# Folding the token mix of the low-rank terms into their weights in an RWKV-7 and stick-breaking decoder

## The chip, the cores and the metric

One core of one Trainium2 chip. The metric is the device time of one execution in microseconds (us). Engines are named as the profile names them: PE (TensorE matmul), PEld (TensorE weight load), DVE (VectorE), ACT (ScalarE), POOL (GpSimd), SP (the engine that issues most transfers).

## The reference

A two-layer decoder on 1040 tokens (16 meta tokens and 1024 of the input) of width 1024. Layer 0 mixes tokens by RWKV-7, layer 1 by stick-breaking attention; a conv-gated MLP follows each. Only the first step of RWKV-7 is touched by the change:

```python
xx = token_shift(x) - x                       # x: (1040, 1024), normed
xr, xw, xk, xv, xa, xg = [x + xx * mix[i] for i in range(6)]
r = xr @ w_r;  k = xk @ w_k;  v = xv @ w_v    # 1024 x 1024 each
w_log = -softplus(-(w0 + tanh(xw @ w1) @ w2)) - 0.5     # w1: 1024 x 64
a = sigmoid(a0 + (xa @ a1) @ a2)                        # a1: 1024 x 64
g = sigmoid(xg @ g1) @ g2                               # g1: 1024 x 160
```

Each `mix[i]` has one number per channel. The terms of `w1`, `a1` and `g1` are called the low-rank terms here.

## The kernel before

Everything is float32. A product is made of three matmuls in a faster 4-byte format: each operand is split into a high part (an ACT copy into that format) and a low part (a subtraction, on DVE or POOL), and high x high, high x low and low x high are summed in PSUM. Activations lie with channels on the 128 partitions, so 1024 channels are eight blocks (`kt` = 0 to 7), and tokens along the free axis.

`rwkv_project` runs first. It treats the tokens in two segments (`SEGS`): 528 tokens (s = 0; products in two column halves of 264) and 512 (s = 1; one product of 512 columns). `phase0` loads the input, turns it and norms it: the normed blocks of segment 0 stay in SBUF with a zero column ahead (`hn0`), and all go to DRAM (`hn_s`), from where a block with the token before it can be read back (`load_hs`, L332). `norms(1)` and `normed(1)` do the same for segment 1; the latter is called in the midst of the mixing of segment 0 (L758).

For each segment `Mixer` (L339) then makes 48 mixed and split inputs, in the order of `mix_jobs` (L404): first 24 for the low-rank terms (for each kt the mixes 1, 4 and 5, that is w, a, g), then eight each for k, r and v. It is a pipeline of jobs: a load of the block six jobs ahead where it is not there (L362), for the way "d" a POOL subtraction that gives the difference of neighbouring tokens (L369, once per block), a DVE operation that multiplies it by the mix and adds h (L381), an ACT copy to the high part (L391, recorded at L76), and a subtraction for the low part on DVE or POOL (L396). For the way "a" an ACT copy scaled by 1 - mix (L374) and a DVE operation (L386) take the place of L369 and L381. Of the low-rank jobs 12 have their low part on DVE and 12 on POOL; of the others 15 on DVE and 9 on POOL.

`lora_in` (L421) splits the low-rank weights (`split_w`, `weights`), and as each job of the 24 is done, `step` issues its matmuls (L453): three for each column half, for w into 64 rows, for a into 64, for g into 128 and, from the second part of `g1`, 32. That is 192 matmuls of 264 columns in segment 0 and 96 of 512 in segment 1. `finish` (L467) applies tanh and sigmoid and splits the results.

Then `first_pair` (L700) makes the mixes of k, r and v and, of eight pairs of heads (128 output columns each), the first: `proj` (L543) for k, r and v, 48 matmuls each in segment 0 and 24 in segment 1, and the second low-rank products (`lora_wa`, `lora_g`). Pairs 1 to 7 follow (`pair`, L669), each beside `stage_e` (L565) of the pair before, which turns k, r, v, w, a into the operands of the recurrence with DVE, ACT, POOL and a few matmuls. `stage_e` of pair 7 of segment 0 runs beside the low-rank part of segment 1 (`next(e)`, L756). In the last pair of segment 0, `tick` (L767) lets the mixer of segment 1 make two steps at each of four places.

What sets the order: all matmuls that go through `pmm` stay in program order on PE. The other engines' queues are ordered by a planner at build time, and buffers are rings by tag: tag "M" holds 24 mixed and split inputs (k, r and v of a segment need all 24 until its last pair), tag "H" 22 vectors of 529 columns, and the tags "wf", "wh" and "wl" two blocks of weights each. After the projections (near 645 us of the span) come the recurrence, the rest of layer 0, layer 1 and the output, which the change does not touch.

Of the kernel before, what the change touches and what calls it, by code (L numbers as in the profile page):

```python
# [51 lines left out]
def kernel(ctx: ExitStack, tc: tile.TileContext, a: dict, out: bass.AP):  # L52
# [141 lines left out]
    NS = 528  # L194
    NC = 8
# [14 lines left out]
    def rwkv_project(ap, pa):  # L210
# [24 lines left out]
        def phase0():  # L235
# [5 lines left out]
            def big(name, n):  # L241
                return ap.tile([P, 2 * NS], F32, tag="M", bufs=24, name=name)[:, 0:n]

# [95 lines left out]
        class Mixer:  # L339
# [10 lines left out]
            def advance(self):  # L350
# [12 lines left out]
                if at(3):  # L363
                    nm, i, kt, via, sub = self.jobs[t + 3]
                    hs = self.hs[nm, kt]
                    if via == "d":
                        if (nm, kt) not in self.dd:
                            dd = H(f"dd{s}{nm}{kt}")[:, 0:n]
                            G.tensor_tensor(dd, hs[:, 0:n], hs[:, 1 : n + 1], op=ALU.subtract)  # L369
                            self.dd[nm, kt] = dd  # L370
                    else:
                        x = H(f"mt{s}{i}{kt}")[:, 0:n]
                        m = i * 8 + kt
                        S.activation(x, hs[:, 1 : n + 1], AF.Copy, scale=der[:, m : m + 1])  # L374
                        self.st[t + 3]["x"] = x
                if at(2):
                    nm, i, kt, via, sub = self.jobs[t + 2]
                    hs, st, m = self.hs[nm, kt], self.st[t + 2], i * 8 + kt
                    if via == "d":
# [7 lines left out]
                if at(1):  # L387
                    nm, i, kt, via, sub = self.jobs[t + 1]
                    st = self.st[t + 1]
                    st["xm"] = xm = ap.tile([P, 2, NS], F32R, tag="M", bufs=24, name=f"xm{s}{i}{kt}")  # L390
                    copy_act(xm[:, 0, 0:n], st["x"])  # L391
                if at(0):
# [3 lines left out]
                    sub.tensor_tensor(xm[:, 1, 0:n], st["x"], f(xm[:, 0, 0:n]), op=ALU.subtract)  # L396
# [24 lines left out]
        def lora_in(s, out):  # L421
# [3 lines left out]
            W = {}  # L425
            acc = {}

            def weights():
                wf = WP["pool"].tile([P, KT, P], F32, tag="wf", name=f"wf_wa{s}")
                nc.sync.dma_start(wf[:, :, 0:64], wview(a["rw_w1"][0], 0, 64))  # L430
                nc.sync.dma_start(wf[:, :, 64:128], wview(a["rw_a1"][0], 0, 64))
                W["wa"] = split_w(wf, P, f"wa{s}")
                wf = WP["pool"].tile([P, KT, P], F32, tag="wf", name=f"wf_g1{s}")
                nc.sync.dma_start(wf, wview(a["rw_g1"][0], 0, P))
                W["g"] = split_w(wf, P, f"g1{s}")
                wf = WP["pool"].tile([P, KT, 32], F32, tag="wf", name=f"wf_g1b{s}")
                nc.sync.dma_start(wf, wview(a["rw_g1"][0], P, 32))
                gh = ap.tile([P, KT, 32], F32R, tag="g1bh", name=f"g1bh{s}")
                gl = ap.tile([P, KT, 32], F32R, tag="g1bl", name=f"g1bl{s}")
                with behind(*begun) if s == 0 else nullcontext():  # L440
                    copy_act(gh, wf)
                    V.tensor_tensor(gl, wf, f(gh), op=ALU.subtract)
                W["gb"] = (gh, gl)
                fs = [ps_l] * 4 if len(hv) == 1 else [ps_l] * 4 + [ps_d] * 3 + [ps_n]
                for c0, cn in hv:
                    for nm in "wagb":
                        acc.setdefault(nm, []).append(fs.pop(0)(f"p{nm}{s}{c0}"))

            def add(nm, m, w, m0, X, kt):
                wh, wl = W[w]  # L450
                for h, (c0, cn) in enumerate(hv):
                    for j, (ww, xx) in enumerate(((wh, X[0]), (wh, X[1]), (wl, X[0]))):
                        pmm(  # L453
                            acc[nm][h][0:m, 0:cn], ww[:, kt, m0 : m0 + m], xx[:, c0 : c0 + cn],
                            start=kt == 0 and j == 0, stop=kt == KT - 1 and j == 2,
                        )

            def step(i, kt, X):
                if i == 1:
                    add("w", 64, "wa", 0, X, kt)  # L460
                elif i == 4:
                    add("a", 64, "wa", 64, X, kt)
                else:
                    add("g", P, "g", 0, X, kt)
                    add("b", 32, "gb", 0, X, kt)

            def finish():  # L467
# [4 lines left out]
                for h, (c0, cn) in enumerate(hv):  # L472
                    cs = slice(c0, c0 + cn)
                    S.activation(tw[0:64, cs], acc["w"][h][0:64, 0:cn], AF.Tanh)
                    copy_act(ta[0:64, cs], acc["a"][h][0:64, 0:cn])
                for h, (c0, cn) in enumerate(hv):
                    cs = slice(c0, c0 + cn)
                    S.activation(tg[:, cs], acc["g"][h][:, 0:cn], AF.Sigmoid)
                    S.activation(tb[0:32, cs], acc["b"][h][0:32, 0:cn], AF.Sigmoid)
# [10 lines left out]
            return weights, step, finish  # L490
# [178 lines left out]
        def pair(s, p, cd, lora, X, e, tick):  # L669
# [30 lines left out]
        def first_pair(s, cd, mixer, lora, lora_finish, X):  # L700
            def mixes(nm, n):
                for got in mixer.finish(n):
                    if got:
                        X[got[0]].append(got[3])
                        yield

            with behind(*begun) if s == 0 else nullcontext():
                load_l2(0, s, cd)
            for i, _ in enumerate(mixes("k", 32)):
                if i == 1:  # L710
                    lora_finish()
            prep(0, s, cd, "k")
            prep(0, s, cd, "r")
            m = mixes("r", 40)
            for _ in proj(0, s, cd, "k", X["k"]):
                for _ in range(4):
                    next(m, None)
            for _ in m:
                pass
            prep(0, s, cd, "v")  # L720
            m = mixes("v", 48)
            for _ in proj(0, s, cd, "r", X["r"]):
                for _ in range(4):
                    next(m, None)
            for _ in m:
                pass
            nx = {}
            for _ in lora_wa(0, s, cd, lora):
                pass
            for _ in lora_g(0, s, cd, lora):  # L730
                pass
            prep(1, s, nx, "k")
            load_l2(1, s, nx)
            for _ in proj(0, s, cd, "v", X["v"]):
                pass
# [8 lines left out]
        mixer = Mixer(0, mix_jobs(), hn0)  # L744
        done = []
        for s in range(2):
            lora, X = {}, {nm: [] for nm in "krv"}
            weights, lora_step, lora_finish = lora_in(s, lora)
            weights()
            for got in done:  # L750
                lora_step(*got[1:])
            for got in mixer.finish(24):
                if got:
                    lora_step(*got[1:])
                    if got[1] == 5:
                        next(e, None)  # L756
                        if got[2] == 3:
                            next(first, None)  # L758
# [3 lines left out]
            nx = first_pair(s, cd, mixer, lora, lora_finish, X)  # L762
            done = []
            if s == 0:
                mixer = Mixer(1, mix_jobs())

            def tick():  # L767
                for _ in range(2):
                    got = mixer.advance()
                    if got:  # L770
                        done.append(got)

            for p in range(1, NP):
                e = stage_e(p - 1, s, cd)
                cd = nx
                nx = pair(s, p, cd, lora, X, e, tick if (s, p) == (0, NP - 1) else lambda: None)
# [1762 lines left out]
```

## Time and profile before

| | |
|---|---|
| time, median of 3 runs | 3629.34 us (3625.01 to 3632.36) |
| the profiled execution's own time | 3628.45 us |
| its span, first to last instruction | 3626.7 us |
| PE busy | 3120.0 us (86%) |
| DVE busy | 2329.0 us (64%) |
| POOL busy | 1735.9 us (48%) |
| ACT busy | 1554.7 us (43%) |
| mean granted TensorE clock | 0.911 |

The span is what the profile shows; the own time is longer by 1.75 us, which lie around it. Times inside the trace are counted from the start of the span. Busy shares are averages over the whole program; the projections, where the change is, fill the first 645 us.

### The profile page before, as it was taken

To read this page: it belongs to the slowest core of one execution; us is meant where nothing else is said; L and a number is where in the kernel's file an instruction comes from. 1 tells how busy PE (TensorE), PEld (TensorE's weight loads), DVE (VectorE), ACT (ScalarE), POOL (GpSimd) and SP (SyncE) were. 2 spreads that over 40 slices of the span, in tenths; PEclk is the share of its full clock that TensorE was granted. 3 is DMA by queue.
4 is the path that set the end of the run, shared out by engine and by line. 5 is a ranking of instruction groups with operands and counts; after the bars stand their busy time and mean duration, and the time that the engine had idled before them with its cause. 6 is when DMAs were issued, how large, how long until landed. Compare 5 with 4: busy or idle time off the path is not lost.

```text
span 3626.7 us, 62709 instructions
## 1 busy us (share of the span) xinstructions
PE 3120.0 (86%) x25101; PEld 2913.6 (80%) x25101; DVE 2329.0 (64%) x3128; ACT 1554.7 (43%) x2859; POOL 1735.9 (48%) x1678
## 2 busy tenths in 40 slices
PE   4798688567778979999899988888889699998998
PEld 4796466456667969999899978788878699998998
DVE  8778866523333588888733377777774988887342
ACT  4664545133335333333333266666654333334232
POOL 5555634344535564454422366666644544444231
PEclk7898799768777989999999999999999799999999
DMA  6344333433335422222445200110035222224453
GB/s 202 104 152 140 123 122 116 119 94 98 106 99 156 138 65 77 83 71 80 150 137 167 90 27 24 27 30 24 21 108 168 90 79 77 77 81 138 122 170 94
DMA packets 439454, 366.61 MB, mean 101 GB/s; under 512 B 66855, under 2 KB 359485, under 8 KB 438907
## 3 DMA queue, kind: packets, MB, share of 16 engines
q1 hardware_dynamic: 438299, 361.28, 33.0%
q8 instruction: 197, 3.23, 0.4%
q0 software_dynamic: 864, 1.33, 0.1%
q14 instruction: 94, 0.77, 0.1%
HBM read 266.51 MB, written 96.02 MB: 100 GB/s over the span
## 4 chain that ended last, share of the span: by engine, by line
PE 45%; DVE 20%; DMA 9%; ACT 6%; issue 5%; POOL 4%; SPq 2%; ACTq 0%; DVEq 0%; POOLq 0%
PE dn L1517 12%; DVE t L1700 5%; DVE om L2254 2%; PE kps L2099 2%; DVE rs L1625 2%; DMA AD<-Aa 2%; PE c L797 1%; POOL be L2257 1%; SPq L44 1%; ACT t L1698 1%; PE wt L2102 1%; PE kp L217 1%; DMA XD<-XL 1%; PE av L2099 1%; PE A L797 1%
## 5 line engine op out<-in xcount | busy, mean ns | idle before, releaser
L1517 PE MATMUL dn<-act,h_dn 128*128 128x260 f32 x2688 | 437.5, 284 | 4.8 <-ACT act L76 2.4
L1517 PEld LDWEIGHTS dn<-act,h_dn 128*128 128x128 f32 x2688 | 373.5, 190 | 5.8 <-ACT act L76 2.8
L1700 DVE SCALAR_TENSOR_TENSOR t<-u,pcol,t 128x1040 f32<-128x1040 f32 x168 | 303.4, 1806 | 108.9 <-ACT t L1698 108.9
L1517 PE MATMUL dn<-act,l_dn 128*128 128x260 f32 x1344 | 273.4, 285 | 1.7 <-POOL l_dn L1466 1.7
L2257 POOL TENSOR_TENSOR be<-be,om 128x911 f32<-128x911 f32 (+7 forms) x128 | 195.8, 1530 | 131.1 <-DVE om L2254 106.6
L1466 POOL TENSOR_TENSOR l_dn<-r_dn,h_dn 128x1024 fp32r<-128x1024 f32 (+1 forms) x46 | 102.5, 2228 | 323.5 <-ACT h_dn L76 322.8
L2254 DVE TENSOR_TENSOR_SCAN om<-om 128x912 f32<-128x912 f32 (+7 forms) x128 | 214.0, 1672 | 49.2 <-POOL om L2249 30.4
L1715 POOL TENSOR_TENSOR t<-t,t 128x1040 f32<-128x1040 f32 x42 | 102.5, 2440 | 253.4 <-DVE t L1700 253.4
L76 ACT ACTIVATE h_dn<-r_dn 128x1024 fp32r<-128x1024 f32 (+1 forms) x92 | 90.7, 986 | 298.2 <-PE dn L1517 276.7
L1517 PEld LDWEIGHTS dn<-act,l_dn 128*128 128x128 f32 x1344 | 207.3, 189 | 2.2 <-POOL l_dn L1466 2.2
L1466 POOL TENSOR_TENSOR s34l<-rs,s34h 128x1024 fp32r<-128x1024 f32 x44 | 105.8, 2404 | 101.1 <-ACT s34h L76 101.1
L76 ACT ACTIVATE WT<-wt 128x512 fp32r<-128x512 f32 (+2 forms) x224 | 98.8, 443 | 117.1 <-PE wt L2102 88.8
L797 PE MATMUL A<-ARz,BK 128*128 128x128 f32 x512 | 91.3, 326 | 58.9 <-DMA ARz<-AR_s 34.1
L2320 DVE TENSOR_TENSOR WT<-wt,WT 128x512 fp32r<-128x512 f32 (+2 forms) x224 | 107.6, 488 | 51.6 <-ACT WT L76 48.2
L2099 PE MATMUL av<-WT,VS 128*128 128x256 f32 (+3 forms) x640 | 108.7, 283 | 32.9 <-DVE WT L2320 32.7
L76 ACT ACTIVATE s34h<-rs 128x1024 fp32r<-128x1024 f32 x44 | 46.7, 1062 | 202.2 <-PE p110S L1652 5.0
L1466 DVE TENSOR_TENSOR l_dn<-r_dn,h_dn 128x1024 fp32r<-128x1024 f32 (+1 forms) x46 | 52.0, 1131 | 122.6 <-ACT h_dn L76 122.5
L2102 PE MATMUL wt<-ident,be 128*128 128x128 f32 x576 | 99.2, 295 | 33.6 <-DVE WTm L2295 33.5
L797 PEld LDWEIGHTS A<-ARz,BK 128*128 128x128 f32 x512 | 75.6, 224 | 65.2 <-issue 34.8
L217 PE MATMUL kp<-xm,wh_rw_wk 128*128 128x264 f32 (+1 forms) x384 | 109.0, 376 | 19.1 <-DVE xm L396 10.5
L2249 POOL TENSOR_SCALAR_AFFINE_SELECT be<-be 128x128 f32<-128x128 f32 x128 | 78.0, 610 | 90.0 <-ACT be L2244 90.0
L2099 PEld LDWEIGHTS av<-WT,VS 128*64 128x64 f32 (+1 forms) x640 | 85.5, 165 | 44.0 <-DVE WT L2320 42.9
(2105 smaller groups left out, 11090.1 us busy)
## 6 DMA issues: line engine op xcount, KB each, us to landing
r_dn<-in_ffn_down_dram SPq DMA_DIRECT2D x60, 512.0 KB
a_s<-t SPq DMA_DIRECT2D x84, 260.0 KB
rv<-in_ffn_up_dram SPq DMA_DIRECT2D x42, 512.0 KB
ra<-in_ffn_up_dram SPq DMA_DIRECT2D x42, 512.0 KB
araw<-a_s SPq DMA_DIRECT2D x50, 260.0 KB
r_dn<-in_ffn_down_dram SPq DMA_DIRECT2D x32, 384.0 KB
raw<-a_s SPq DMA_DIRECT2D x36, 260.0 KB
hr<-h_s SPq DMA_DIRECT2D x32, 260.0 KB
```

Source lines behind the costliest of these rows:

```text
L76: return S.activation(o, i, AF.Copy, scale=scale)
L217: return tc.keep_in_program_order(mm(*args, **kw))
L797: return tc.keep_in_program_order(mm(*args, **kw))
L1466: eng.tensor_tensor(lo, x, f(hi), op=ALU.subtract)
L1517: self.mm(ps[:, c, :], w[:, kk, :], X[k][i][:, c * CH : (c + 1) * CH], start=k == 0 and j == 0, stop=k == len(X) - 1 and j == 2,)
L1700: VV.scalar_tensor_tensor(t[j], u[j][:, i : i + n], w, t[j], op0=ALU.mult, op1=ALU.add)
L1715: (G if n == L else VV).tensor_tensor(t[1], t[0], t[1], op=ALU.mult)
L2099: return tc.keep_in_program_order(mm(*args, **kw))
L2102: return tc.keep_in_program_order(nc.tensor.transpose(*args))
L2254: V.tensor_tensor_scan(om[0:nq, 0:nk], om[0:nq, 0:nk], om[0:nq, 0:nk], 1.0, op0=ALU.mult, op1=ALU.min)
L2257: G.tensor_tensor(be[0:nq, 1:nk], be[0:nq, 1:nk], om[0:nq, 0 : nk - 1], op=ALU.mult)
L2320: V.tensor_tensor(wt[:, 1, s0:s1], ps[:, s0:s1], f(wt[:, 0, s0:s1]), op=ALU.subtract)
```

## The change

The mix is linear in h and in the token before it, and has one factor per channel, so that x + (shift(x) - x) m, multiplied by W, is x times (1 - m)W plus shift(x) times mW. The change uses this for the low-rank terms. Instead of 24 mixes in a segment, each split, h itself is split once (eight jobs of the new way "s", 529 columns with the token ahead; the low part on DVE), and the products read it twice: from column 1 on for (1 - m)W, from column 0 on for mW. The weights come in three sets: A (w1 and a1 side by side, 128 columns), B (the first 128 columns of g1) and C (its last 32). `folded` makes for a set mW (a POOL product with the mix broadcast along the columns) and (1 - m)W (a POOL subtraction), and both are split as before. So there are 6 x 8 x 3 products for each column half: 288 matmuls of 264 columns in segment 0 and 144 of 512 in segment 1.

The order changes with it. `steps` issues the products set by set; at every third step the mixer advances by one job, so that the mixes of k and seven of r are issued beside the low-rank products. Set A of segment 1 is folded, and its first half split, in the last pair of segment 0, and there the mixer makes four steps at each of the four places: all eight splits of h and two mixes of k. In `first_pair` the r product comes after `lora_wa` and `lora_g`. For k of segment 0 the blocks `hn0` in SBUF are used and not loaded again.

```diff
+    NM = NS + 2
...
+                    if via == "s":
+                        self.st[t + 3]["x"] = hs[:, 0 : n + 1]
+                    elif via == "d":
...
-                    copy_act(xm[:, 0, 0:n], st["x"])
+                    copy_act(xm[:, 0, 0 : n + (via == "s")], st["x"])
...
-                    sub.tensor_tensor(xm[:, 1, 0:n], st["x"], f(xm[:, 0, 0:n]), op=ALU.subtract)
+                    w = n + (via == "s")
+                    sub.tensor_tensor(xm[:, 1, 0:w], st["x"], f(xm[:, 0, 0:w]), op=ALU.subtract)
...
             for kt in range(KT):
-                for j, i in enumerate((1, 4, 5)):
-                    jobs.append(("l", i, kt, "d", G if j == 1 or (j == 2 and kt % 2) else V))
+                jobs.append(("l", 0, kt, "s", V))
...
+            def folded(name, m, loads, mix):
+
+                wf, w2 = (
+                    WP["pool"].tile([P, KT, m], F32, tag="wf", bufs=2, name=f"wf{j}_{name}{s}") for j in range(2)
+                )
+                for o, src in loads:
+                    nc.sync.dma_start(wf[:, :, o : o + src.shape[2]], src)
+                k = mix.shape[2]
+                v4 = [t.rearrange("p t (k x) -> p t k x", k=k) for t in (w2, wf)]
+                G.tensor_tensor(
+                    v4[0], v4[1], mix.unsqueeze(3).broadcast_to([P, KT, k, m // k]), op=ALU.mult
+                )
+                G.tensor_tensor(wf, wf, w2, op=ALU.subtract)
+                return wf, w2
+
+            def products(nm, m, j, w):
+
+                for kt in range(KT):
+                    for h, (c0, cn) in enumerate(hv):
+                        o = c0 + 1 - j
+                        for i, (ww, x) in enumerate(((w[0], 0), (w[0], 1), (w[1], 0))):
+                            pmm(
+                                acc[nm][h][0:m, 0:cn], ww[:, kt, 0:m], HL[kt][x][:, o : o + cn],
+                                start=j + kt + i == 0, stop=j == 1 and kt == KT - 1 and i == 2,
+                            )
+                    yield
+
+            def steps():
...
+                A1 = split_w(fA[0], P, f"A1{s}")
+                yield
+                A2 = split_w(fA[1], P, f"A2{s}")
+                yield
+                fs = [ps_l] * 4 + [ps_d] * 2
...
+                yield from products("A", P, 0, A1)
+                mixg = pcol[:, mb + 40 : mb + 48].unsqueeze(2)
+                fB = folded("B", P, ((0, wview(a["rw_g1"][0], 0, P)),), mixg)
+                B1 = split_w(fB[0], P, f"B1{s}")
+                yield from products("A", P, 1, A2)
+                B2 = split_w(fB[1], P, f"B2{s}")
+                yield from products("B", P, 0, B1)
+                fC = folded("C", 32, ((0, wview(a["rw_g1"][0], P, 32)),), mixg)
...
+                yield from products("B", P, 1, B2)
+                yield from products("C", 32, 0, C[0])
+                yield from products("C", 32, 1, C[1])
...
             for _ in proj(p, s, cd, "r", X["r"]):
                 step()
                 tick()
+            after_r()
...
+            prep(0, s, cd, "k")
+            lora_finish()
+            prep(0, s, cd, "r")
             for _ in proj(0, s, cd, "k", X["k"]):
+                advance(4)
             prep(0, s, cd, "v")
             for _ in lora_wa(0, s, cd, lora):
                 pass
             for _ in lora_g(0, s, cd, lora):
                 pass
+            for _ in proj(0, s, cd, "r", X["r"]):
+                advance(4)
...
+            advance(40)
             for _ in proj(0, s, cd, "v", X["v"]):
                 pass
...
+        for kt in range(KT):
+            hn0["k", kt] = hn0["l", kt]
...
+            advance(40, KT)
+            for i, _ in enumerate(steps):
+                if i % 3 == 0:
+                    advance(1, 3 * KT - 1)
+                if i % 6 == 2:
+                    next(e, None)
+                if i == 8:
+                    next(first, None)
...
             def tick():
-                for _ in range(2):
-                    got = mixer.advance()
-                    if got:
-                        done.append(got)
+                seg[4](4, KT + 2)
```

## Rows read from the trace of the kernel before

**Rows 1.** The page: busy time, share of the span, instructions.
```profile
PE 3120.0 (86%) x25101; PEld 2913.6 (80%) x25101; DVE 2329.0 (64%) x3128; ACT 1554.7 (43%) x2859; POOL 1735.9 (48%) x1678
```

**Rows 2.** Busy time of each engine: the two low-rank stretches, the pairs.
```profile
core 0: us, PE busy (x) PEld busy (x) DVE busy (x) ACT busy (x) POOL busy (x), PEclk, DMA share, GB/s
43.00:146.00 103.00, 58.32 (x332) 50.32 (x331) 97.61 (x92) 55.19 (x99) 70.92 (x39) 0.75 0.37 119
326.00:446.00 120.00, 74.03 (x228) 43.18 (x227) 115.63 (x127) 57.81 (x95) 77.21 (x49) 0.72 0.39 120
...
146.00:326.00 180.00, 179.63 (x1353) 170.47 (x1353) 125.07 (x237) 102.12 (x190) 88.29 (x63) 0.98 0.47 145
```

**Rows 3.** Who waited for whom, 43 to 153 us: total, times, longest.
```profile
ACT xm L76 <- DVE mt L381: 33.7, 15, 10.7
PE pg L217 <- DVE xm L396: 19.4, 3, 11.5
```

**Rows 4.** The same view, 320 to 450 us.
```profile
ACT xm L76 <- DVE mt L381: 51.3, 20, 7.9
```

**Rows 5.** PE in order of time: the first k product of pair 1, either segment.
```profile
152.25 0.50 PE L217 MATMUL kp<-xm,wh_rw_wk 128*128 128x264 f32 x2
...
446.40 1.05 PE L217 MATMUL kp<-xm,wh_rw_wk 128*128 128x512 f32 x2
```

**Rows 6.** Durations (ns min/median/max) at L381 and L396, 43 to 146 us.
```profile
L381 DVE SCALAR_TENSOR_TENSOR mt<-dd0l,pcol,hn x24: 754/758/1835, 43.6 to 84.6; 128x528 f32<-128x528 f32 x24
...
L396 DVE TENSOR_TENSOR xm<-mt,xm x27: 695/700/2859, 47.0 to 140.8; 128x528 fp32r<-128x528 f32 x27
L396 POOL TENSOR_TENSOR xm<-mt,xm x21: 1473/1765/3174, 46.6 to 144.1; 128x528 fp32r<-128x528 f32 x21
```

**Rows 7.** DVE busy with L381 alone (second stretch, then first, of the low-rank mixing).
```profile
331.00:388.00 57.00, 24.86 (x24) 0.73 0.39 120
43.00:86.20 43.20, 27.79 (x24) 0.74 0.45 142
```

**Rows 8.** DVE and POOL busy with L396 alone, either stretch.
```profile
43.00:146.00 103.00, 31.74 (x27) 40.14 (x21) 0.75 0.37 119
326.00:446.00 120.00, 33.29 (x27) 34.19 (x21) 0.72 0.39 120
```

**Rows 9.** DVE groups of 43 to 145 us: the split of the small weights.
```profile
L442 DVE TENSOR_TENSOR g1bl<-wf_g1b,g1bh 128x256 fp32r<-128x256 f32 x1 | 1.3, 1283 | 0.0
```

**Rows 10.** Busy time in the last pair of segment 0.
```profile
300.00:326.00 26.00, 26.00 (x201) 24.67 (x200) 19.59 (x37) 13.91 (x26) 13.52 (x11) 1.00 0.55 166
```

**Rows 11.** POOL groups, 0 to 145 us: a weight split, differences of tokens.
```profile
L418 POOL TENSOR_TENSOR wl_g<-wf_g,wh_g 128x1024 fp32r<-128x1024 f32 x1 | 2.3, 2337 | 0.0
...
L369 POOL TENSOR_TENSOR dd0r<-hs00r 128x528 f32<-128x528 f32 x1 | 1.1, 1062 | 0.0
```

**Rows 12.** PE in order of time: 264 columns at half, then at full clock.
```profile
68.13 0.64 PE L217 MATMUL pb<-xm,g1bh 128*32 128x264 f32 x2
68.57 0.42 PE L217 MATMUL pb<-xm,g1bl 128*32 128x264 f32 x1
68.79 0.64 PE L217 MATMUL pb<-xm,g1bh 128*32 128x264 f32 x2
...
97.40 0.41 PE L217 MATMUL pa<-xm,wh_wa 128*64 128x264 f32 x2
97.65 0.28 PE L217 MATMUL pa<-xm,wl_wa 128*64 128x264 f32 x1
97.77 0.41 PE L217 MATMUL pa<-xm,wh_wa 128*64 128x264 f32 x2
```

**Rows 13.** PE in order of time: 512 columns at full clock.
```profile
357.80 0.62 PE L217 MATMUL pa<-xm,wh_wa 128*64 128x512 f32 x2
358.26 0.40 PE L217 MATMUL pa<-xm,wl_wa 128*64 128x512 f32 x1
358.50 0.62 PE L217 MATMUL pg<-xm,wh_g 128*128 128x512 f32 x2
```

**Rows 14.** Weight loads of k (ns min/median/max), whole trace.
```profile
L217 PEld LDWEIGHTS kp<-xm,wh_rw_wk x384: 186/188/338, 101.0 to 627.0; 128*128 128x128 f32 x192
```

**Rows 15.** ACT groups, 43 to 145 us: the high part of a weight block.
```profile
L76 ACT ACTIVATE wh_rw_wr<-wf_rw_wr 128x1024 fp32r<-128x1024 f32 x1 | 1.0, 1048 | 0.0
```

**Rows 16.** SP's queue, 25 to 145 us: a weight load that waited for its buffer.
```profile
SPq L153 <- POOL wl_rw_wk L161: 22.6, 2, 14.7
```

More of the change, by code (lines that the diff above doesn't have):

```diff
@@ L419, in split_w, with lora_in @@
             return wh, wl
-        def lora_in(s, out):
+        def lora_in(s, out, HL):
             n = SEGS[s][1]
             hv = cols(s)
-            W = {}
             acc = {}
[L428 to L444, printed above, removed]
@@ L445, in weights @@
+            def steps():
+                fA = folded(
+                    "A", P, ((0, wview(a["rw_w1"][0], 0, 64)), (64, wview(a["rw_a1"][0], 0, 64))),
+                    pcol[:, mb + 8 : mb + 56].rearrange("p (k x) -> p x k", k=2)[:, 0:KT],
+                )
+                A1 = split_w(fA[0], P, f"A1{s}")
[3 more added lines that the diff above has]
+                fs = [ps_l] * 4 + [ps_d] * 2
                 for c0, cn in hv:
-                    for nm in "wagb":
+                    for nm in "ABC":
@@ new lines, in steps @@
+                B1 = split_w(fB[0], P, f"B1{s}")
[3 more added lines that the diff above has]
+                fC = folded("C", 32, ((0, wview(a["rw_g1"][0], P, 32)),), mixg)
+                C = []
+                for j in range(2):
+                    ch, cl = H(f"C{j}{s}", F32R)[:, 0 : 2 * KT * 32].rearrange("p (i t m) -> i p t m", i=2, t=KT)
+                    copy_act(ch, fC[j])
+                    G.tensor_tensor(cl, fC[j], f(ch), op=ALU.subtract)
+                    C.append((ch, cl))
@@ L488, in finish @@
                 out.update(LW=LW, GH=GH, G3=G3)
-            return weights, step, finish
+            return steps(), finish
         def load_l2(p, s, cd):
@@ L743, in rwkv_project, with begin, advance @@
         begun = hn0.pop("first")
-        mixer = Mixer(0, mix_jobs(), hn0)
-        done = []
-        for s in range(2):
[L747 to L758, printed above, removed]
+        for kt in range(KT):
+            hn0["k", kt] = hn0["l", kt]
+        def begin(s, hs=None):
+            mixer = Mixer(s, mix_jobs(), hs)
+            X, lora = {nm: [] for nm in "lkrv"}, {}
+            steps, finish = lora_in(s, lora, X["l"])
+            def advance(n, last=4 * KT):
+                for _ in range(n):
+                    if mixer.t < last:
+                        got = mixer.advance()
+                        if got:
+                            X[got[0]].append(got[3])
+            return X, lora, steps, finish, advance
+        seg = begin(0, hn0)
+        next(seg[2])
+        for s in range(2):
+            X, lora, steps, lora_finish, advance = seg
+            next(steps)
+            advance(40, KT)
[6 more added lines that the diff above has]
+                    next(first, None)
             for _ in e:
@@ L775, in rwkv_project @@
                 cd = nx
-                nx = pair(s, p, cd, lora, X, e, tick if (s, p) == (0, NP - 1) else lambda: None)
+                end = (s, p) == (0, NP - 1)
+                nx = pair(
+                    s, p, cd, lora, X, e, tick if end else lambda: None, (lambda: next(seg[2])) if end else lambda: None
+                )
             e = stage_e(NP - 1, s, cd)
```

64 lines of the change are left out of this document (15 added, 49 removed).

## The prediction

> **What bounds the kernel now.** The profile's page comes first: PE is busy for 86% of the span and DVE, the next engine, for 64%, so on the average PE is the bound [rows 1]. The change, however, touches two stretches only, so the busy time by stretches is read next [rows 2]. In the pairs of segment 0 (146 to 326 us) PE works 179.6 of 180 us at a granted clock of 0.98. In the two stretches with the low-rank mixing it does not: 58.3 of 103 us and 74.0 of 120 us, at 0.75 and 0.72, that is, about half of the time at either level, 1.2 and 2.4 GHz. DVE is the full engine there: 97.6 of 103 and 115.6 of 120 us. POOL has 70.9 and 77.2 us, ACT under 60 in both. The view of waits says who waits for DVE: ACT's split copies for the DVE mix (33.7 us and 51.3 us in total), PE for DVE's low parts, once for 11.5 us [rows 3, 4]. The stretches end where the first k product of pair 1 starts, at 152.25 and 446.40 us [rows 5]; from there on PE, or a chain that the change leaves alone, sets the pace. So what DVE is spared in these stretches is time, until PE or POOL takes over.
>
> How dear is a DVE operation there? A mix alone takes 0.758 us and a low part 0.700 us (medians), yet some take 1.8 and 2.9 us [rows 6]: the long ones lie beside POOL work. What counts is the mean as it stands in the stretch, with that delay in it: 27.79 / 24 = 1.16 us a mix, 31.74 / 27 = 1.18 us a low part in segment 0; 24.86 / 24 = 1.04 and 33.29 / 27 = 1.23 us in segment 1 [rows 7, 8].
>
> **The change part by part.**
>
> *DVE, segment 0.* The 24 mixes go: 27.8 us. Of low parts, 12 go and 8 come: 4 x 1.18 = 4.7 us. The small weights' low part goes to POOL: 1.3 us [rows 9]. Together 33.8 us of a full engine. One column more in a split (529 of 528) is nothing.
>
> *DVE, segment 1.* 24.9 + 4 x 1.23 + 1.3 = 31.1 us. Besides, eight splits and two k mixes move into the last pair of segment 0. They cost some 10 low parts (12.3 us) and 2 mixes (2.1 us), and DVE has 26.0 - 19.6 = 6.4 us free there [rows 10], beside a PE that is full. I count those 6.4 us as gained and the rest as backlog of `stage_e` that is carried over the border: 37.5 us. The sum of both segments is 71.3 us.
>
> *POOL.* Gone in a segment: 12 low parts (40.14 / 21 = 1.91 us each, 22.9 us; in segment 1 1.63 us, 19.5 us), eight differences (1.1 us and more each [rows 11]) and two weight splits. New: two operations for each folded set and two splits, for A and B of 1024 elements. The trace shows no POOL product with a broadcast operand. Its floor is two differences of 528, 2.1 us, its ceiling the weight split with its delays, some 2.8; I take the nearest, the undelayed split, 2.34 us [rows 11]. A and B then cost 8 x 2.34 = 18.7 us and C, a quarter as wide with four operations, 2.4, of which A's 9.4 lie ahead of the mixing in segment 0. POOL falls to near 48 us there and 60 in segment 1, below what is left for DVE. ACT loses 16 copies and gains two large ones. Neither becomes the bound by this.
>
> *PE.* 288 matmuls for 192 and 144 for 96. Three of 264 columns start within 0.37 us at full clock, 0.123 us each, and within 0.66 at half, 0.22 each [rows 12]; three of 512 within 0.70, 0.233 each [rows 13]. So PE has 96 x 0.123 = 11.8 and 48 x 0.233 = 11.2 us more work. PE has some 45 us free in either stretch, so this costs nothing while DVE ends last. If DVE were no matter at all, PE's own line would be: segment 0 from 44.4 (one copy, one subtraction): 48 products at half clock 10.6, 240 at full 29.5, then k, r and v, 144 x 0.123 = 17.7, some 4 for the second low-rank products and some 6 until v's last mix: 112 us for 152.25, a gain of 40. By DVE's sum it is 118, so both are close and DVE's stands. Segment 1 from 329: 33.6 for the low-rank products, 4.5 for `stage_e`'s, 6 for late weights, 16.8 for k, r and v, 2.5: 392 us for 446.4, a gain of 54; DVE's sum gives 409.
>
> The weight load of 128 columns lasts 0.188 us [rows 14] beside the spacing of 0.123, so it lies under the matmuls. The Trainium skill (TensorE: Matmul & The Clock Gate, The mechanism) speaks against the change here: it says that weight loads overlap running matmuls only where they go to other row groups. By that each product would cost 0.188 more, and PE's line in segment 0 would grow by 288 x 0.188 = 54 us to 166, beyond today's 152; the measured spacing says otherwise, and I give that case no chance.
>
> *Reads from column 1.* Half of the products read an operand that starts one element later, at an odd column. No matmul of this trace is known to do so. From below nothing; from above half rate, 144 x 0.1 = 14 us and 72 x 0.233 = 17 us of PE time, which takes PE's lines to 126 and 409. I take nothing: DVE's L386 and L381 read the token before and the token itself from such columns at the undelayed 0.758 us.
>
> *Queues.* The ring of two for "wf" is full while a set is folded, and "wh" frees a block only when its products are done. B1 must be split within the eight steps of A's second half (48 x 0.123 = 5.9 us) by an ACT copy of 1.05 us [rows 15] and 2.34 on POOL behind at most one other operation: about even, a few us late at worst, and DVE's line covers that. SP issues 16 block loads in the last pair of segment 0 for three before; behind a weight load that waits for its buffer (14.7 us once [rows 16]) they would be late, and their cover is the PE work of that pair. The k blocks of segment 0 are no longer loaded. `normed(1)` stands in the midst as before.
>
> *Sum.* 3628.45 - 71.3 = 3557.2 in the profiled execution's terms, which is 0.9 below the median of the runs: 3558.
>
> **The rivals.**
>
> *PE's own lines are reached.* If DVE's remaining operations also get shorter, since POOL has 23 and 17 us less to do beside them, the ends fall to 112 and 392: a gain of 40 + 54 = 94, 3535. For it: the delayed operations [rows 6]. Against: the 35 us of backlog and mixing in segment 1 that POOL work still lies beside. Chance 0.19.
>
> *PE stays at half clock in segment 0.* The clock was 0.75 there, with gaps; the new products come close together, as in the pairs, where it was 0.98 [rows 2]. Should some late weights keep it low, 288 + 144 products at 0.22 are 95 us and with 44.4 and 10 for the rest the end is 149: gain 3, and 37.5 in segment 1: 3589. Chance 0.11.
>
> *DVE and POOL take strict turns.* Then a stretch lasts as long as both engines' undelayed work together. In segment 0 that is 24 x 0.758 + 23 x 0.700 + about 13 of other DVE work, 47 us, and 9 x 1.06 + 9 x 1.47 + 4 x 2.34 + 11.8 on POOL, 44 us: to 43 + 91 + 6 for the last products = 140, a gain of 12, likewise some 13 in segment 1: 3604. Against: by this the stretch today would hold 48 x 0.758 + 27 x 0.700 + 13 = 68 and 17 x 1.06 + 21 x 1.47 + 4 x 2.34 = 58 us, 126 in all, and it took 103. Chance 0.04. The Trainium skill has this as a rule (SBUF — State Buffer, SBUF: two separate sides): the port pair that the two engines share is an exclusive lock for a whole instruction with two SBUF inputs. By that rule it is 3604; the trace agrees in kind (1.83 us for 0.76) and not in full.
>
> *Slower: the rings of weights stall PE.* Sets B and C are refilled in either segment while PE, in its fixed order, can only wait. At its dearest a refill has a wait as in [rows 16] (14.7), a fold (4.7) and two splits one after the other (2 x 3.4), 26 us, less the 5.9 of one running half set: 20 us, four times 80 us, 3638 with the other gains given. It decides the sign from 18 us a refill. For it: the row was seen. Against: it stood behind mixes on POOL that are nearly halved. Chance 0.04.
>
> *The change does not do what it says for the time*: what is saved up to 645 us is lost in the recurrence behind it, since that waits for something else; 3628. Against: PE's first recurrence work waits for data of the projections. Chance 0.02.
>
> **How the numbers follow.** The forecast, DVE's sum, has 0.60, with a range of its own of 3540 to 3580 (the odd columns, late weights). About 0.2% (7.3 us) is what a measurement of this kernel can tell from no change. Faster: 0.60 + 0.19 + 0.11 + 0.04 = 0.94; same 0.02; slower 0.04. The range takes in the first three cases with the bounds of the unknown prices: 3528 to 3596.
>
> **What would show it.** Right: L381 runs 18 times (9 a segment, for k, r and v) and not 66; pair 1's first k product starts near 118 us in segment 0 and near 375 (446 less 71) in segment 1; PE's granted clock in both stretches above 0.85; DVE below 95% there. Wrong: a PE that waits for POOL's or ACT's weight splits of B and C (the rings), a spacing of 0.22 us in products from column 1 (odd columns), DVE still full with the same number of us (strict turns), or an unchanged end of the projections.

## The result and the profile after

The changed kernel takes 3574.45 us (median of 4 runs, 3569.47 to 3580.96), against 3629.07 of the kernel before in 4 runs beside it: a ratio of 0.985, 95% interval 0.9832 to 0.9868, that is 54.6 us or 1.5% faster. The forecast was 3558. In the two profiled executions the spans differ by 50.3 us (3576.4 for 3626.7), and on these the account below is made.

The page first, the line that answers to [rows 1]:

```profile
PE 3111.6 (87%) x25245; PEld 2922.6 (82%) x25245; DVE 2281.0 (64%) x3070; ACT 1538.7 (43%) x2833; POOL 1708.1 (48%) x1658
```

DVE has 58 instructions and 48 us less, POOL 20 and 28 us less, PE 144 more, as the change says. Where the time went is seen at the marks of [rows 5], the first k product of pair 1 in either segment. PE in order of time, changed kernel (start and duration in us):

```profile
124.64 0.41 PE L218 MATMUL kp<-xm0k,wh_rw_wk 128*128 128x264 f32 x2
...
396.98 0.63 PE L218 MATMUL kp<-xm1k,wh_rw_wk 128*128 128x512 f32 x2
```

The first mark came 27.6 us earlier (33.8 forecast), the second 49.4 (71.3 forecast), so segment 1 with the last pair before it gave 21.8 where 37.5 were expected. Behind the second mark little is added: the span as a whole is 50.3 us shorter.

The busy time in the stretches that end at the marks (each second stretch begins 147.75 us behind the first mark, so it holds the last pair of segment 0 too). Before:

```profile
core 0: us, PE busy (x) PEld busy (x) DVE busy (x) ACT busy (x) POOL busy (x), PEclk, DMA share, GB/s
43.00:152.25 109.25, 64.20 (x358) 56.21 (x358) 98.69 (x94) 56.20 (x101) 71.23 (x39) 0.73 0.38 120
300.00:446.40 146.40, 100.43 (x427) 68.16 (x426) 135.22 (x163) 71.91 (x122) 90.73 (x59) 0.77 0.42 128
```

After:

```profile
43.00:124.64 81.64, 64.16 (x452) 60.40 (x453) 73.19 (x63) 44.30 (x80) 56.02 (x31) 0.87 0.40 126
272.40:396.98 124.58, 98.31 (x478) 76.17 (x478) 111.99 (x135) 64.83 (x110) 80.04 (x50) 0.88 0.48 153
```

DVE is still the fullest engine, 90% busy in both, with 25.5 and 23.2 us less busy time. PE does 94 and 51 products more in the same busy time, because the clock rose from 0.73 and 0.77 to 0.87 and 0.88. POOL's operations fell only by 8 and 9 in number: most of what the mixing gave up there came back as folds and splits of weights. What PE waits for in segment 0 (43 us to the mark):

```profile
PE rep_n L289 <- DVE dg_n L286: 9.4, 1, 9.4
PE rp L218 <- ACT G L76: 2.1, 1, 2.1
PE pB L218 <- POOL wl_B L423: 2.0, 1, 2.0
PE kp L218 <- POOL wl_rw_wk L161: 1.9, 1, 1.9
PE pB L218 <- ACT wh_B L76: 1.7, 1, 1.7
PE pC L218 <- ACT C L76: 1.0, 1, 1.0
PE pC L218 <- POOL C L486: 0.8, 1, 0.8
```

The waits for DVE's low parts of [rows 3] are gone. One wait for DVE is left, and it stands ahead of the first low-rank product: PE waits 9.4 us for the operand of a small norm product and starts the low-rank work at 51.9 us. Behind it the view puts none of PE's waits in segment 0 down to DVE; the 9.5 us that are left go to copies and splits by ACT and POOL. The work just before that start shows why, DVE in order of time:

```profile
39.41 0.71 DVE L402 TENSOR_TENSOR xm0l<-hn,xm0l 128x529 fp32r<-128x529 f32 x1
...
40.24 8.40 DVE L402 TENSOR_TENSOR xm0l<-hn,xm0l 128x529 fp32r<-128x529 f32 x4
```

and POOL in order of time:

```profile
39.62 5.47 POOL L423 TENSOR_TENSOR wl_A<-wf_A,wh_A 128x1024 fp32r<-128x1024 f32 x2 [10.40 <-ACT wh_A L76]
45.05 3.02 POOL L372 TENSOR_TENSOR dd0k<-hn 128x528 f32<-128x528 f32 x2
```

The first row is a split of one eighth of h that begins with POOL idle, 0.2 us ahead of POOL's next operation: 0.71 us. The next four, in the very 8.4 us in which POOL splits set A and makes two differences, take 2.1 us each. A later spot shows the two engines taking turns, one operation each. DVE in order of time:

```profile
87.45 1.57 DVE L391 SCALAR_TENSOR_TENSOR mt<-hs05r,pcol,mt 128x528 f32<-128x528 f32 x1
88.94 1.57 DVE L391 SCALAR_TENSOR_TENSOR mt<-hs07r,pcol,mt 128x528 f32<-128x528 f32 x1
```

POOL over the same stretch:

```profile
84.05 1.06 POOL L372 TENSOR_TENSOR dd0r<-hs03r 128x528 f32<-128x528 f32 x1
...
86.93 1.53 POOL L372 TENSOR_TENSOR dd0r<-hs06r 128x528 f32<-128x528 f32 x1
88.42 1.53 POOL L372 TENSOR_TENSOR dd0v<-hs00v 128x528 f32<-128x528 f32 x1
```

At 84.05 DVE was idle and the difference took 1.06 us; beside DVE it takes 1.53, and DVE's mix 1.57 for its 0.76. From 86.93 to the end of the last DVE row 3.6 us pass, and 2 x 1.06 + 2 x 0.76 is 3.64. By these durations both show as busy while one of them waits for the other. From 43 us to the second mark all 33 DVE operations of the mixing (L386, L391, L402) that took over 0.85 us began while a POOL operation ran, and 52 of the 55 quicker ones began while none did. That made the question for the experiments: is DVE's delay a property of DVE's operations, as the forecast priced it (1.16 us for a mix of 0.758), or of POOL's?

### The profile page after: what moved, and what is told of

It reads as the page before. It is cut to its first block, busy times and chain, and to the rows that moved or that the text cites. A ratio compares the mean times of both kernels' runs of the same rounds, so it can differ in the third digit from the quotient of the medians.

```text
span 3576.4 us, 62819 instructions
## 1 busy us (share of the span) xinstructions
PE 3111.6 (87%) x25245; PEld 2922.6 (82%) x25245; DVE 2281.0 (64%) x3070; ACT 1538.7 (43%) x2833; POOL 1708.1 (48%) x1658
## 3 DMA queue, kind: packets, MB, share of 16 engines
q0 software_dynamic: 864, 1.33, 0.1%
## 4 chain that ended last, share of the span: by engine, by line
PE 29%; DVE 10%; POOL 4%; ACT 3%; issue 3%; DMA 2%; SPq 0%; ACTq 0%; POOLq 0%; DVEq 0%
PE dn L1544 12%; DVE t L1727 3%; DVE om L2281 2%; PE kps L2126 2%; PE wt L2129 1%; PE av L2126 1%; POOL be L2284 1%; PE qps L2126 1%; PE sop L2126 1%; DMA araw<-a_s 1%; DVE rs L1652 1%; PE z L2126 1%; POOL be L2276 1%; PE vps L2126 1%; ACT t L1725 1%
## 5 line engine op out<-in xcount | busy, mean ns | idle before, releaser
L2129 PEld LDWEIGHTS wt<-ident,be 128*128 128x128 f32 x576 | 80.0, 155 | 40.0 <-DVE WTm L2322 36.2
```

Of the source, the lines that this page charges most:

```text
L2129: return tc.keep_in_program_order(nc.tensor.transpose(*args))
```

## The experiments

All of them change the kernel after. "Marks" are the two first k products of pair 1, 124.64 and 396.98 us in it; the shift given is that of the second mark. The marks are the measure, because the rest behind them is the same code and yet varies: from the first product of the recurrence to the end of the span it takes 2950 to 2968 us in these traces. Each mark comes from one trace: in runs 3 and 5, whose edits lie behind the first mark, that mark stands 0.2 us before and 1.3 us behind the changed kernel's, so a shift of one or two us says nothing.

| kernel | us, median (range) | ratio to before (95%) | marks | shift |
|---|---|---|---|---|
| changed | 3574.45 (3569.47 to 3580.96) | 0.985 (0.9832 to 0.9868) | 124.64, 396.98 | |
| 1 fold left out | 3557.57 (3556.91 to 3560.79) | 0.9807 (0.9783 to 0.9832) | 117.52, 383.96 | -13.0 |
| 2 own tiles for dg | 3580.2 (3565.27 to 3580.99) | 0.9857 (0.9829 to 0.9885) | 120.77, 392.37 | -4.6 |
| 3 closing step early | 3577.25 (3576.92 to 3580.18) | 0.986 (0.984 to 0.9881) | 124.40, 393.53 | -3.5 |
| 4 low parts all on DVE | 3563.39 (3558.94 to 3571.08) | 0.9823 (0.9799 to 0.9847) | 119.23, 388.70 | -8.3 |
| 5 nothing moved ahead | 3570.42 (3562.26 to 3575.32) | 0.9846 (0.9819 to 0.9874) | 125.95, 396.71 | -0.3 |
| 6 mixes put back | 3596.05 (3589.15 to 3603.26) | 0.9919 (0.9894 to 0.9945) | 138.23, 423.82 | +26.8 |
| 7 edits 2, 3 and 4 | 3556.73 (3551.56 to 3558.01) | 0.9808 (0.9784 to 0.9832) | 119.69, 386.60 | -10.4 |
| 8 POOL's low parts twice | 3588.17 (3586.75 to 3591.31) | 0.9898 (0.9875 to 0.9922) | 136.37, 414.95 | +18.0 |
| 9 no differences on POOL | 3557.0 (3546.38 to 3562.51) | 0.9806 (0.9788 to 0.9824) | 117.00, 383.27 | -13.7 |
| 10 edits 2, 3, 4 and 9 | 3553.24 (3548.79 to 3565.99) | 0.9804 (0.9784 to 0.9824) | 114.26, 374.67 | -22.3 |

**1. The fold left out.** The weights are loaded a second time and split as they are; the factors 1 - m and m of the low-rank weights are left out of the computation.

```diff
...
-                G.tensor_tensor(
-                    v4[0], v4[1], mix.unsqueeze(3).broadcast_to([P, KT, k, m // k]), op=ALU.mult
-                )
-                G.tensor_tensor(wf, wf, w2, op=ALU.subtract)
+                for o, src in loads:
+                    nc.sync.dma_start(w2[:, :, o : o + src.shape[2]], src)
```

> Leaves out the folding: the weights are loaded twice and split as they are, so POOL loses six operations a segment (some 12 us) and nothing else changes. Theory 'the delay belongs to POOL' (DVE loses about 0.25 us for each us of POOL): DVE busy from pair 7 of segment 0 to pair 1 of segment 1 falls from 112 to 108 to 110, the time by 3 to 8 us with the waits for weights that end earlier. Theory of the prediction (a DVE operation has its price whatever POOL does): DVE busy stays at 112, the time falls by 0 to 4 us.

Twelve POOL operations less, none of DVE's, and the marks came 7.1 and 13.0 us earlier; DVE's busy time in the two stretches fell from 185.2 to 174.2 us. All eight splits of h, on DVE, from 40.4 us on (min, median, max in ns; before the edit the last four took 2100 each):

```profile
L402 DVE TENSOR_TENSOR xm0l<-hn,xm0l x8: 693/698/708, 40.4 to 45.9; 128x529 fp32r<-128x529 f32 x8
```

With POOL quiet there, no split is delayed, and PE's first low-rank product starts at 48.0 for 51.9. The fold that was priced at no time, because POOL isn't the bound, costs 13 us. In segment 0 the way through DVE is seen, in the four splits and the late start behind them; in segment 1 it is argued from DVE's shorter busy time, and weights that are ready earlier without the fold were not told apart from it.

**2. Tiles of their own for the operand that PE waited for.**

```diff
+                dgs = H(f"dgs{gi}")
...
-                        dg = small.tile([P, P], F32, tag="dg", name=f"dg_n0{gi}{g0}{i}")
+                        dg = dgs[:, (g0 + i) * tt : (g0 + i + 1) * tt]
```

> The small diagonal tiles of the first norm get room of their own and no ring of two, so that the second norm's row products can stand ahead of the splits of h. Theory 'PE starts late' (segment 0 lost its 6 us because the first low-rank product waited behind them until 51.9 us): first product near 45 us, pair 1's first k product of segment 0 at 118 to 121 for 124.64, the time 3 to 7 us less. Rival 'DVE ends last' in segment 0: first product earlier, but pair 1 starts at 123 to 125, the time within 2 us.

PE starts at 47.4 for 51.9 and the first mark follows by 3.9 us. So the late start in segment 0 is real time, though not all of it every time: in run 3 PE starts 1.8 us earlier without an edit there, and the mark moves by 0.2. The kernel as a whole shows nothing of it (0.9857 against 0.985): the part behind the projections took 8 us longer in this trace, within its spread.

**3. The closing step of the last pair of segment 0 ahead of the rest of the queue.**

```diff
+            next(e, None)
             advance(40, KT)
```

> The first step of pair 7's second stage (a scan and a square) is issued ahead of the low-rank part of segment 1, so PE's 9.8 us wait for the square should go, or shrink under 3. Theory 'DVE ends last' in segment 1: pair 1 of segment 1 starts within 2 us of 396.98, the time within 2 us. Rival 'PE's fixed order' (its waits add up to the end): pair 1 starts 6 to 10 us earlier and the time falls as much.

The hr_kk product that PE waited 9.8 us for starts at 320.1 for 326.8. The wait itself didn't go: the product stands earlier in PE's order and PE still waits 7.3 us there, and 5.9 for the next product of that step (2.0 before). 3.5 us are left at the mark, between the two expectations, and nothing in the median.

**4. All low parts of k, r and v on DVE.**

```diff
-                    jobs.append((nm, i, kt, "d" if kt % 3 == 0 else "a", G if kt % 3 == 1 else V))
+                    jobs.append((nm, i, kt, "d" if kt % 3 == 0 else "a", V))
```

> All low parts of k, r and v on DVE: nine operations a segment go from POOL to DVE. Theory of the prediction (1.2 us each as it stands in the stretch): DVE busy up by 11 us a segment, the time up by 15 to 22 us. Theory 'the delay belongs to POOL': 6.3 us alone less 0.25 of the 14 us that POOL loses, DVE busy up by 2 to 4 us a segment, the time up by 0 to 7 us, or down, if POOL's queue held others up.

DVE, the fullest engine, got 18 operations more, and its busy time in the two stretches fell from 185.2 to 173.8 us; the marks came 5.4 and 8.3 us earlier. By the forecast's way of pricing it had to be 15 to 22 us slower; the other theory had it about even, and faster only if POOL's queue held others up. The low parts of r and v, most of them with POOL idle, and those of h beside POOL's split of set A:

```profile
L402 DVE TENSOR_TENSOR xm0r<-mt,xm0r x8: 696/699/709, 78.9 to 91.4; 128x528 fp32r<-128x528 f32 x8
L402 DVE TENSOR_TENSOR xm0v<-mt,xm0v x8: 694/696/709, 99.6 to 113.9; 128x528 fp32r<-128x528 f32 x8
L402 DVE TENSOR_TENSOR xm0l<-hn,xm0l x3: 1566/1567/2842, 40.7 to 45.0; 128x529 fp32r<-128x529 f32 x3
```

The same operation is 0.70 us, or 1.57 and 2.84, by what POOL does beside it.

**5. Nothing of segment 1 in the last pair of segment 0.**

```diff
             next(steps)
+            if s == 1:
+                next(steps)
...
             def tick():
-                seg[4](4, KT + 2)
+                pass
```

and the fold of set A at that place in the pair is dropped.

> Nothing of segment 1 is done in the last pair of segment 0 any more: the eight splits, the two k mixes and set A's fold all run from the border on. Step 'free time of the last pair' of the prediction: DVE had 6.4 us free there, so the kernel gets some 6.4 us slower than the changed one (about 3581) and the first k product of pair 1 in segment 1 comes at about 403. Rival that the traces suggest (the moved work has to be paid inside the pair, because DVE idled no less after the change, 12.6 us against 11.2): the pair of segment 0 gets shorter by what the border gets longer, and the mark at 397 moves by less than 4 us either way. Third: set A's fold and split, 8 us of POOL's work and 3 us of transfers, now stand ahead of PE's first low-rank product, which comes 10 us or more later after the pair's end than now (4.5 us), and the kernel is 15 us slower.

The mark moved by 0.3 us, and the median is 4 us lower, within the spread. The second theory holds: the 6.4 us of free DVE time of [rows 10] bought nothing.

**6. The mixes put back on DVE.** Their results are written over.

```diff
+                    if via == "s":
+                        for j in (1, 4, 5):
+                            V.scalar_tensor_tensor(
+                                xm[:, 1, 0:n], st["x"][:, 0:n], pc("mix", j * 8 + kt), st["x"][:, 1 : n + 1],
+                                op0=ALU.mult, op1=ALU.add,
+                            )
```

> Beside the split of each eighth of h, DVE computes the three mixes again that the change took away (their results are written over by the low part and used by nobody): 24 of DVE's operations a segment, with the folded weights and PE's work as they are. The prediction priced each at its mean with delay, 1.16 us: k product of pair 1 in segment 0 from 124.6 to 152, in segment 1 to 452 in all, the kernel some 55 us slower (about 3630). The theory that has come from the traces prices them without delay, at 0.74 to 0.76: 18 us a segment, marks at 143 and 433, the kernel 33 to 40 us slower (about 3610). Rival, that DVE isn't the bound after the change: under 10 us a segment, since the queue waits for PE or POOL anyway. DVE's busy time in the two stretches (73.2 and 112.0 us now) rises by 18 each by the second theory, by 27 each by the first.

48 mixes moved the marks by 13.6 and 26.8 us, 0.56 us each: half of the forecast's 1.16 and 1.04, and below the undelayed 0.74 to 0.76. In segment 0 some 4.5 us of them fell into gaps of DVE (it idles 3.9 us for 8.5). The shift lies between the second theory and the rival. The windows:

```profile
43.00:138.20 95.20, 66.06 (x456) 61.36 (x457) 91.29 (x88) 45.10 (x80) 54.71 (x31) 0.81 0.35 108
286.00:423.80 137.80, 98.82 (x476) 75.08 (x475) 122.95 (x158) 64.84 (x110) 84.98 (x49) 0.83 0.44 134
```

DVE has 25 and 23 operations and 18.1 and 11.0 us more, at the same number of POOL operations: 0.75 and 0.46 us for each of the 24 mixes. They bring hardly any delay of their own.

**7. Edits 2, 3 and 4 together.**

> Three of the single edits together: all low parts of k, r and v on DVE, tiles of their own for the operand of the repetition product, and the first part of pair 7's closing step ahead of the rest of the queue. Alone they brought the first k product of pair 1 in segment 0 to 119.2, 120.8 and 124.4 (124.6 without), and in segment 1 to 388.7, 392.4 and 393.5 (397.0 without). If they add up: 115.5 and 381, and a kernel at about 3552 to 3560. If the first two lift the same wait (DVE's queue ahead of PE's first low-rank product), no better than the best single one: 119 and 388, and 3563. Pairs of 26 or 29 us, which change between runs of one code, move it by up to 8 us either way.

386.6 is better than the best of the three (388.7) by 2 us, little more than a mark varies by, and far from the sum (381). The second case, then: the edits lift waits that stand one behind the other.

**8. POOL's low parts computed twice.**

```diff
+                    if sub is G:
+                        sub.tensor_tensor(xm[:, 1, 0:w], st["x"], f(xm[:, 0, 0:w]), op=ALU.subtract)
                     sub.tensor_tensor(xm[:, 1, 0:w], st["x"], f(xm[:, 0, 0:w]), op=ALU.subtract)
```

> POOL computes each of its low parts (9 of the 24 of k, r and v in a segment) twice, the second time over the first; DVE's operations stay as they are. That is 9 more operations of some 1.7 us on POOL, 15 us a segment. Theory that DVE's delay belongs to POOL's work: DVE's busy time in the two stretches (73.2 and 112.0 us) rises by 0.25 to 0.8 us for each us of POOL's, 4 to 12 us a segment, with the same count of operations, and the kernel is 8 to 24 us slower; this would be the mirror of the run with all low parts on DVE, where DVE's busy time fell by 11 us in all though it got 18 operations more. Rival, that the delay belongs to DVE's own operations (their source or their queue): busy time stays within 2 us, and the time is longer only by PE's waits for POOL.

The marks came 11.7 and 18.0 us later, 1.0 us for each of the 18 operations; the kernel is 14 us slower, as the first theory had it. But the way was the rival's:

```profile
43.00:136.40 93.40, 67.00 (x453) 62.34 (x454) 75.95 (x63) 44.20 (x80) 68.90 (x40) 0.84 0.38 118
284.15:414.90 130.75, 96.42 (x475) 75.11 (x475) 112.28 (x134) 64.10 (x109) 90.95 (x58) 0.86 0.44 140
```

DVE's busy time rose by 2.8 and 0.3 us only. DVE idles instead (17.5 of 93.4 us for 8.5 of 81.6), behind others that wait for POOL's longer queue. In segment 1 PE stands 11.1 us for ACT's copy of set C, and ACT 4.2 of them for POOL's fold:

```profile
PE pC L218 <- ACT C L76: 11.1, 1, 11.1
ACT C L76 <- POOL wf_C L448: 4.2, 1, 4.2
```

**9. The differences of neighbouring tokens off POOL.** All mixes go the way that 15 of 24 go, over ACT; DVE's operations are the same in number and length.

```diff
-                    jobs.append((nm, i, kt, "d" if kt % 3 == 0 else "a", G if kt % 3 == 1 else V))
+                    jobs.append((nm, i, kt, "a", G if kt % 3 == 1 else V))
```

> All mixes of k, r and v go the way that 15 of 24 go already (ACT scales h, DVE adds the shifted h times the mix), so POOL's 9 differences of neighbouring tokens in a segment are gone; DVE has the same number of operations of the same length (0.758 and 0.760 us undelayed), ACT 9 more. A clean test of the price of a POOL operation beside a full DVE. If a POOL operation holds DVE up for its own undelayed length (1.06 us) where both have work, DVE's busy time in the two stretches (73.2 and 112.0 us) falls by 7 to 9.5 us each, and the k products of pair 1 come near 117 and 383 instead of 124.6 and 397.0; the kernel is some 12 us faster than the changed one, 3562. If DVE's delay is 0.13 to 0.46 us for each us of POOL's (13 us fewer a segment), it falls by 2 to 6 us each and the kernel is 3 to 10 us faster. Third: ACT, with 9 scaled copies more in a queue that already holds up PE's hr_kk product, takes the gain back: no faster than 3574.

117.00 and 383.27, where the first theory had 117 and 383. The windows:

```profile
43.00:117.00 74.00, 63.27 (x453) 60.02 (x454) 61.85 (x63) 49.56 (x89) 44.51 (x22) 0.89 0.45 141
264.75:383.30 118.55, 95.84 (x478) 74.34 (x477) 101.52 (x135) 69.96 (x119) 68.45 (x40) 0.90 0.50 158
```

The counts of DVE are the same as after the change, 63 and 135, and it is busy 11.3 and 10.5 us less. That is 1.2 to 1.3 us for each POOL operation that is gone, somewhat over its undelayed 1.06. One caution: runs 2, 3 and 5 took away no operation at all and have 7 to 10 us less DVE time in both stretches together than the changed kernel, presumably by the way the two queues happen to meet; of the 21.8 us here so much may be luck. The marks, 13.7 us earlier or 0.76 for each operation, are the safer price.

**10. Edits 2, 3, 4 and 9 together.**

> The three edits of the combined run (3556.7, marks 119.7 and 386.6) and the differences of POOL gone as well. POOL has then only weights to split and fold in the low-rank stretches. If POOL's operations still are what stretches DVE's, marks near 114 and 378 and 3545 to 3550. If PE's own work and the waits that are left in its order (7.7 us before the first low-rank product, the hr_kk product in segment 1) end the stretches now, no change: 3553 to 3560.

The marks are the first theory's (114 and 378), another 11.9 us before those of run 7 for 18 POOL operations less, 0.66 each. The median gained 3.5 us only, since the part behind the projections took 2966 us in this trace and the runs spread from 3549 to 3566. It has the lowest median of all kernels here, 3553.24, with run 9, a change of one line, beside it (0.9804 and 0.9806); both are faster than the kernel before and, by intervals that don't meet, than the changed one.

## Why the prediction came out as it did

**What held.** The direction and the place: both stretches got shorter, DVE was the bound before, and the clock rose above 0.85 in both (0.87, 0.88). L386, the old L381, runs 18 times. DVE is below 95%. Reads from column 1 cost nothing: three products of 264 columns of set A's first half follow each other in 0.37 us at full clock, as in [rows 12]. PE in order of time, changed kernel:

```profile
57.05 0.41 PE L218 MATMUL pA<-xm0l,wh_A 128*128 128x264 f32 x2
57.30 0.29 PE L218 MATMUL pA<-xm0l,wl_A 128*128 128x264 f32 x1
57.42 0.41 PE L218 MATMUL pA<-xm0l,wh_A 128*128 128x264 f32 x2
```

The weight loads stayed under the matmuls, and the rings cost little: PE waits 3.7 us for the splits of set B and 1.8 for those of set C in segment 0, where the rival needed 18 us a refill. The rival with the half clock in segment 0 didn't come.

**The step that failed: "What counts is the mean as it stands in the stretch, with that delay in it."** 1.16 and 1.04 us a mix gave 52.7 us for the 48 mixes. Put back, they cost 26.8 (run 6). The delay in that mean belonged to POOL's operations and stays when DVE's go; it then falls on DVE's remaining ones, as on the four splits that took 8.4 us.

**Its counterpart: POOL's operations at nothing.** "Neither becomes the bound by this" was right of the busy time (POOL has 56.0 of 81.6 and 80.0 of 124.6 us), and the wrong question. By DVE's delay (run 4) or by the engines that wait for POOL's queue (run 8), a POOL operation costs 0.66 to 1.0 us at the marks (runs 8, 9 and 10 against 7; run 4 gives the same: 8.3 us earlier although 18 operations at 0.56 were added to DVE, so 18.4 us for 18 off POOL). The change took 24 low parts and 16 differences off POOL, by that price 26 to 40 us of gain, and put the fold on it, 13.0 us of loss (run 1), besides four more splits of weights in each segment, two of them of the small set C. With 26.8 for the mixes and 8 x 0.56 = 4.5 for DVE's own low parts, the sum is 45 to 58 us before those splits are taken off; 49.4 were measured. These prices were taken one by one, and run 7 shows that savings need not add up, so the sum is an estimate. By it the forecast was near because two errors opposed each other: DVE's operations at twice their price, POOL's at none, in both directions.

**The 6.4 us of the last pair** were not there (run 5). DVE had free time on the average of that pair, but no work that ended earlier moved the mark.

**PE's start in segment 0** was taken as 44.4 us and was 51.9, behind the delayed splits; runs 1 and 2 start it some 4 us earlier. From its first product to the mark PE needs 72.7 us after the change, where the forecast's own line for PE had 112 - 44.4 = 67.6. The difference, 5.1 us, is about PE's waits for sets B and C (5.5), and 112, 7.5 of later start and 5.5 of these waits make 125 for 124.64 measured. So in segment 0 the end fits PE's own line and what POOL and ACT hand to it, with DVE 90% busy beside it; but the terms are rough, since run 4 has 3.7 us of such waits and needs 67.5. The rival in which PE's lines are reached was right as to how: runs 4, 9 and 10, with less POOL work, need 67.5 to 68.5 us and run 1, without the fold, 69.6. Run 7 needs 72.0, though, and no first mark here comes before 114.26, where that rival had 112.

**The rival of strict turns** had 0.04 and was weighed by the sum of both engines, which didn't fit: 126 us of work in 103. Taken one meeting at a time it fits: 2 x 1.06 + 2 x 0.76 in 3.6 us. The Trainium skill (SBUF — State Buffer, SBUF: two separate sides) has it so, a lock held for the whole instruction while the other engine blocks; the trace agrees here, for DVE operations with two inputs. What the sum missed is not shown; one reason may be that it counted POOL's low parts at 1.47 us, and one with DVE idle takes 1.33 in run 9. The Trainium skill also says (Perfetto Trace Analysis, Optimizing Scalar/DVE Operations) that moving work between these two engines might not help. Run 4 differs: moving 18 low parts from POOL to DVE brought the second mark 8.3 us forward. A likely reason, not tried by itself, is that the operation is 0.70 us on DVE and 1.33 or more on POOL, so that it holds the other engine up for less time.

What stays open: the four more splits of weights in each segment have no experiment of their own, how much of a POOL operation's price goes by either of the two ways is not told apart, and why the unchanged part behind the projections takes 2950 in one trace and 2968 in another was not tried.

## What to carry to other kernels

Where DVE and POOL work beside each other, price an operation of either at its undelayed time at most, and charge a POOL operation to the stretch as well, even if POOL is far from full: here removing one counted, and adding one did too, by way of DVE's delay or of the engines that wait for POOL's queue. Look at the spread of one form's durations (0.70, 1.57, 2.84 us) before taking a mean: here its levels went with what ran on the other engine at the time. And measure at a mark near the change; the median of a long program can hide 10 us of it.

## What was not expected of the hardware

The same operation on data of the same shape is 0.70 us or 2.1 us on DVE, by POOL's being idle or not, and the profile shows both engines as busy meanwhile. Giving 18 operations more to the engine that was 90% busy brought its end forward, by 8.3 us at the second mark (run 4). DVE's busy time for one and the same list of operations varied from 175.6 to 185.2 us over both stretches (run 5 and the changed kernel) with the second mark only 0.3 us apart, so a busy time isn't a path even on the fullest engine.
